# New transfer costs and a new precedence table for a statically scheduled two-block kernel

## The chip, the cores and the metric

The kernel runs on one core of a Trainium2 chip. The metric is the device time of one execution in microseconds (us); the number that counts is the median over runs.

## The reference

Two transformer-like blocks of width 1024 over one sequence of 256 tokens, in float32:

```python
def first_block(x, c, ...):
    mod = silu(c) @ ada_w + ada_b                     # six vectors of 1024
    u = modulate(rmsnorm(x, g), sh_mix, sc_mix)
    p = u @ w_in
    y_conv = conformer_conv(p[..., :1024], ...)       # gated depthwise conv, 31 taps
    y_rwkv = rwkv7_mix(p[..., 1024:], ...)            # 8 heads of 64, a recurrence over the tokens
    x = x + gt_mix * (concatenate([y_conv, y_rwkv]) @ w_out)
    u = modulate(rmsnorm(x, g2), sh_ffn, sc_ffn)
    x = x + gt_ffn * peer_ffn(u, w_q, sub_keys, peer_u, peer_v)
    return rmsnorm(x, final_g)

def peer_ffn(u, ...):     # 8 heads; top 16 of 128 keys twice, top 16 of their 256 sums
    ...                   # picks among 16384 experts with rows in peer_u and peer_v
    h = gelu(einsum('thkd,td->thk', peer_u[expert], u))
    return einsum('thk,thkd->td', softmax(best) * h, peer_v[expert])

def second_block(x, c, ...):
    mod = silu(c) @ w_mod + b_mod
    proj = modulate(rmsnorm(x), ...) @ w_in           # q, k, v of two attentions, an index, gates
    merged = sigmoid(ga) * (dsa(...) @ w_br_dsa) + sigmoid(gb) * (moba(...) @ w_br_moba)
    x = x + gt_m * (merged @ w_out)
    g, up = split(modulate(rmsnorm(x), ...) @ w_gate_up)
    return x + gt_f * ((silu(g) * up) @ w_down)
```

## The kernel before

The program is written as a plain list of operations, and a planner decides where each one stands. `Recorder` notes every operation with the tiles that it reads and writes. `Schedule` is a list scheduler: it plays the five queues PE, ACT, DVE, POOL and DMA forward in model time, gives each operation the duration that `cost` returns, lets its readers become ready after a latency (`latency`, and `DMA_LAT` behind a transfer), and whenever a queue is free takes the ready operation with the highest precedence. Precedence (`bl`) is the length of the longest chain behind the operation in the model, plus its entries in the table `PRIORITY`, one for the stage ("mods3") and one for stage, operation and tile ("mods3 dma_start wraw"), in ns. A positive entry also counts for everything ahead of the operation, a negative one for it alone. The planner also picks the buffer, and for casts and some arithmetic the engine (ACT or DVE, DVE or POOL). What comes out is an order for each queue; the chip then runs each queue in that order, every instruction waiting on semaphores. `build` writes it through one helper line, so every instruction of the program has line 696 in the trace, and rows are told apart by tile names.

All transfers are issued from SP's queue, which is in order too: a transfer that waits for its source or for its buffer holds all those behind it. Four kinds matter below.

- Weights: blocks of 128x1024 floats (512 KB) into `W_wraw`, three buffers (`WRAW = 3`). Each is cast to a rounded high part `W_whi` (on ACT or DVE), the rest goes to `W_wlo` (DVE, seldom POOL), and every product is made of three matmuls. The buffer is free again when `W_wlo` is done.
- Scratch: arrays `scrn0..3` and `scrx0..3` in DRAM, through which the RWKV part rearranges blocks: `scrn` is written from `Ach_AB` in `chunk_first` and read into `Ach_nblk` in `base`; `scrx` is written from `Ach_ublk` in `base` and read into `Arw_XT` in `chunk_mats`.
- Rows: `row_bcast` writes a vector of 1024 that lies as 128x8 in SBUF to DRAM (`row02`, `row05`, `row12`, `row15`, 4 KB each, one element at a time), and reads it back on all partitions. The first, of stage "row", has its source from the modulation stage "mods2".
- Modulation weights: `in_adaR` blocks in the stages "mods2" to "mods4", used directly by matmuls.

In time the stages are: norm, projections and RWKV of block one with the rest of its modulation (0 to 230 us), PEER queries and top-k (`topk`, to some 410), the expert products `hidden` over `peer_u` (to 720), `values` over `peer_v` with the second block's modulation beside them (to 1080), and the second block, whose token-major products `tok_skew` (24 matmuls of 512 columns for two token tiles and one weight block, first one token tile, then the other) stand at its begin and at the begin of its FFN (1285 to 1335).

Of the kernel before, what the change touches and what calls it, by code (L numbers as in the profile page):

```python
# [17 lines left out]
DMA_LAT = 950.0  # L18
# [187 lines left out]
def cost(op, out, reads):  # L206
    n = _free(out)
    if op.eng == "PE":
# [4 lines left out]
        m = _free(lhs)  # L213
# [16 lines left out]
    if op.eng == "DMA":  # L230
        b = P * n * 4
        return b / 358.0 - 8
# [507 lines left out]
def _real(x):  # L740
# [51 lines left out]
    "add C01 scalar_tensor_tensor nsc": -6000.0,  # L792
    "add C01 tensor_mul gtmp": 2500.0,
    "add E00": 35000.0,
    "add E00 tensor_mul gtmp": 82500.0,
    "add E00 tensor_tensor xres": -14000.0,
    "add E01": 3500.0,
    "add E01 scalar_tensor_tensor nsc": -36000.0,
    "add E01 tensor_mul gtmp": -56000.0,
    "add E01 tensor_tensor xres": -145500.0,  # L800
    "attend00 copy ohi": -2000.0,
    "attend00 copy pT": -12000.0,
    "attend00 matmul n": -2000.0,
    "attend00 matmul p": -1000.0,
    "attend00 reciprocal asum": -2000.0,
    "attend00 tensor_mul lg0": -8000.0,
    "attend00 tensor_scalar amax": -3000.0,
    "attend00 tensor_sub olo": 2000.0,
# [3 lines left out]
    "attend01 reciprocal asum": -14000.0,  # L812
# [4 lines left out]
    "attend01 transpose r": 500.0,  # L817
    "attend10 matmul n": -16000.0,
    "attend10 matmul p": -2000.0,
    "attend10 reciprocal asum": 1000.0,  # L820
    "attend10 tensor_reduce amax": -3500.0,
    "attend10 tensor_scalar amax": 16000.0,
    "attend10 tensor_sub olo": -3000.0,
    "attend11 activation lg1": -4000.0,
# [7 lines left out]
    "base": 17500.0,  # L832
    "base dma_start dram": 500.0,
    "base dma_start nblk": -13500.0,
    "base memset ublk": -16000.0,
    "base tensor_mul ublkp": -57000.0,
    "base tensor_reduce ublk": 22500.0,
    "bonus matmul m": -26500.0,
    "bonus tensor_mul av": -1000.0,
    "bonus tensor_scalar av": -4000.0,  # L840
    "consts activation cvec": 40000.0,
    "consts dma_start clevf": -1500.0,
    "consts dma_start cmask": 10000.0,
    "consts dma_start cvec": -16000.0,
    "consts dma_start lorawa": 30000.0,
    "consts dma_start xres": 2000.0,
    "consts iota pj": -125500.0,
    "consts memset bd64": -43000.0,
    "consts memset bdones": -4500.0,
    "consts memset eps": -16000.0,  # L850
    "consts memset o512": -13500.0,
    "consts memset zero": -71000.0,
    "consts tensor_copy clev": -32000.0,
    "consts tensor_scalar ident": 1000.0,
    "consts tensor_scalar omka": 34000.0,
    "conv": -4000.0,
    "conv activation cacc": -18000.0,
    "conv activation convy": 1000.0,
    "conv activation lnr": 1000.0,
    "conv activation tableout": -41000.0,  # L860
    "conv reciprocal lnr": -2000.0,
    "conv tensor_mul cacc": 1500.0,
    "conv tensor_mul lnr": -2500.0,
    "conv tensor_mul lnt": 7000.0,
    "conv tensor_scalar cacc": 9000.0,
    "conv tensor_scalar lnt": -1000.0,
    "conv tensor_scalar lnvv": -41000.0,
    "conv tensor_sub cacc": 1000.0,
    "conv transpose x": 2000.0,
    "ffn activation fsilu": 500.0,  # L870
    "ffn activation ftok": 17000.0,
    "ffn copy whi": -1500.0,
    "ffn dma_start row": -19000.0,
    "ffn dma_start wraw": -4000.0,
    "ffn matmul h": -3000.0,
    "ffn tensor_mul fsilu": -33000.0,
    "ffn tensor_mul ftok": 30500.0,
    "ffn transpose r": -2000.0,
    "ffn0": -500.0,
    "ffn0 dma_start wraw": -15000.0,  # L880
    "ffn0 tensor_tensor wlo": -500.0,
    "ffn1": 500.0,
    "ffn1 copy whi": -15500.0,
    "ffn1 dma_start wraw": -4000.0,
    "ffn1 matmul c": -500.0,
    "ffn1 tensor_tensor wlo": -2000.0,
    "final0": -5000.0,
    "final0 activation f1s": 2000.0,
    "final0 activation f2s": 61000.0,
    "final0 activation mraw": 2000.0,  # L890
    "final0 reciprocal f1r": 3000.0,
    "final0 reciprocal f2r": 6000.0,
    "final0 scalar_tensor_tensor f1t": 32000.0,
    "final0 scalar_tensor_tensor f2t": 36000.0,
    "final0 tensor_add fw": 11000.0,
# [3 lines left out]
    "final0 tensor_scalar f1t": -20000.0,  # L899
    "final0 tensor_scalar f2t": -6000.0,  # L900
    "final0 tensor_scalar xres": -2000.0,
    "final0 tensor_tensor xres": -1000.0,
    "final1 activation f1s": -24000.0,
    "final1 activation f2s": -15500.0,
# [4 lines left out]
    "final1 tensor_mul f1r": 4000.0,  # L909
    "final1 tensor_scalar f1e": -16000.0,  # L910
    "final1 tensor_scalar f1t": -4500.0,
    "final1 tensor_scalar fv": -2000.0,
# [4 lines left out]
    "first0 matmul a": 42000.0,  # L917
    "first0 scalar_tensor_tensor ZR": 4000.0,
    "first0 tensor_mul AB": -12500.0,
    "first0 tensor_mul ZR": -3500.0,  # L920
    "first0 tensor_tensor W": -15000.0,
    "first0 tensor_tensor ZR": 4000.0,
    "first1 dma_start dram": 500.0,
    "first1 matmul b": -39000.0,
    "first1 scalar_tensor_tensor ZR": -1500.0,
    "first1 tensor_mul AB": 8500.0,
    "first1 tensor_mul ZR": -9000.0,
    "first1 tensor_tensor W": -16500.0,
    "first1 tensor_tensor ZR": -4000.0,
    "first2": -9500.0,  # L930
    "first2 dma_start dram": -10500.0,
    "first2 matmul a": 30000.0,
    "first2 scalar_tensor_tensor ZR": -44000.0,
    "first2 tensor_mul AB": -1000.0,
    "first2 tensor_mul ZR": 54500.0,
    "first2 tensor_tensor W": -1000.0,
    "first2 tensor_tensor ZR": 16000.0,
    "first3": 32000.0,
    "first3 dma_start dram": -44500.0,
    "first3 matmul b": -8000.0,  # L940
    "first3 scalar_tensor_tensor ZR": -39500.0,
    "first3 tensor_mul AB": -49500.0,
    "first3 tensor_mul ZR": -4000.0,
    "first3 tensor_tensor W": -12000.0,
    "first3 tensor_tensor ZR": -1000.0,
# [3 lines left out]
    "gn0 activation gsq": 9000.0,  # L949
    "gn0 matmul m": 2000.0,  # L950
    "gn0 reciprocal gnr": -55000.0,
    "gn0 scalar_tensor_tensor yr": -8000.0,
    "gn0 tensor_mul gno": -1000.0,
    "gn0 tensor_mul gnt": -183000.0,
    "gn0 tensor_mul yr": -59500.0,
    "gn0 tensor_scalar gvar": -82000.0,
    "gn0 tensor_sub yr": -12500.0,
    "gn0 transpose m": -56500.0,
    "gn1": 3500.0,
    "gn1 activation gnr": -3000.0,  # L960
    "gn1 activation gsq": -3000.0,
    "gn1 matmul m": -14500.0,
    "gn1 reciprocal gnr": -2000.0,
    "gn1 scalar_tensor_tensor yr": 14500.0,
    "gn1 tensor_mul gno": 32000.0,
    "gn1 tensor_mul yr": 17500.0,
    "gn1 tensor_scalar gnt": 2000.0,
    "gn1 tensor_scalar gvar": -39000.0,
    "gn1 tensor_sub yr": 7500.0,
    "gn1 transpose m": -27500.0,  # L970
    "hidden0 dma_start wraw": -48000.0,
# [3 lines left out]
    "hidden1 copy whi": -4000.0,  # L975
    "hidden1 dma_start wraw": 8000.0,
    "hidden1 matmul h": 3000.0,
    "hidden1 tensor_tensor wlo": 1000.0,
    "hidden2": -1000.0,
    "hidden2 activation gH0": 10000.0,  # L980
    "hidden2 activation gel": -8000.0,
    "hidden2 copy whi": -16000.0,
# [5 lines left out]
    "hidden3 activation gel": -500.0,  # L988
    "hidden3 dma_start wraw": 500.0,
    "hidden3 matmul h": -8000.0,  # L990
# [3 lines left out]
    "hidden4 activation gel": 20000.0,  # L994
    "hidden4 copy whi": 12000.0,
    "hidden4 dma_start wraw": -14000.0,
    "hidden4 matmul h": -29000.0,
    "hidden4 tensor_tensor gH1": 500.0,
    "hidden4 tensor_tensor wlo": 1000.0,
    "hidden5 activation gH1": -2000.0,  # L1000
    "hidden5 matmul h": -16000.0,
    "hidden5 tensor_tensor gH1": 16000.0,
    "hidden6 activation gH1": -7000.0,
# [6 lines left out]
    "hidden7": -2000.0,  # L1010
    "hidden7 activation gH1": 7000.0,
    "hidden7 activation gel": 33000.0,
    "hidden7 copy whi": 9000.0,
    "hidden7 dma_start wraw": 1000.0,
    "hidden7 matmul h": -18500.0,
    "hidden7 tensor_tensor gH1": 17000.0,
    "hidden7 tensor_tensor wlo": 500.0,
    "index copy ki": -18000.0,
# [7 lines left out]
    "index memset kz": 16000.0,  # L1026
# [3 lines left out]
    "index tensor_scalar wi": -2000.0,  # L1030
    "index tensor_sub ropeO": 3000.0,
    "index tensor_tensor ropeB": 6000.0,
    "index transpose r": -16500.0,
    "mats0 copy WT": -20000.0,
    "mats0 copy X": -49000.0,
    "mats0 copy Ylev": -8000.0,
    "mats0 copy_predicated X": 9500.0,
    "mats0 copy_predicated XT": 5000.0,
    "mats0 dma_start XT": 5000.0,
    "mats0 matmul a": -93500.0,  # L1040
    "mats0 transpose a": -32000.0,
    "mats1": -2500.0,
    "mats1 copy WT": -31000.0,
    "mats1 copy X": -134000.0,
    "mats1 copy Ylev": -13500.0,
    "mats1 copy_predicated X": 8500.0,
    "mats1 copy_predicated XT": -36000.0,
    "mats1 dma_start XT": 6000.0,
    "mats1 transpose b": 5500.0,
    "mats2 copy WT": -15000.0,  # L1050
    "mats2 copy X": 26500.0,
    "mats2 copy Ylev": 1000.0,
    "mats2 copy_predicated X": -29000.0,
    "mats2 copy_predicated XT": -22000.0,
    "mats2 dma_start XT": -57000.0,
    "mats2 matmul a": -1500.0,
    "mats2 transpose a": -16000.0,
    "mats3": 8500.0,
    "mats3 copy X": 7000.0,
    "mats3 copy Ylev": 7000.0,  # L1060
    "mats3 copy_predicated X": -39500.0,
    "mats3 copy_predicated XT": -46000.0,
    "mats3 dma_start XT": -30500.0,
    "mats3 matmul b": -56500.0,
    "mats3 transpose b": -4000.0,
    "merge": -1000.0,
    "merge activation tableout": -7000.0,
    "merge copy chi": -14000.0,
    "merge copy whi": -25500.0,
    "merge dma_start wraw": -8000.0,  # L1070
    "merge tensor_add mg": -1000.0,
    "merge tensor_sub clo": -3000.0,
    "merge tensor_tensor wlo": -1000.0,
    "mods2": 1000.0,
    "mods2 copy modrows": -21500.0,
    "mods2 dma_start hraw": -8000.0,
    "mods2 dma_start wraw": 2000.0,
    "mods2 tensor_add mod": -25000.0,
    "mods2 transpose m": 2000.0,
# [1934 lines left out]
```

## Time and profile before

| | |
|---|---|
| median of 3 runs | 1500.91 us (1496.61 to 1501.64) |
| the profiled execution, its own time | 1507.02 us |
| its span, first to last instruction | 1505.2 us |
| PE, PEld, DVE, ACT, POOL busy | 1432.8, 1252.0, 1258.5, 511.3, 97.8 us |
| mean granted TensorE clock | 0.988 |

PE is the matmul engine and PEld its weight loads, which overlap it; DVE, ACT and POOL are the vector, scalar and general engines, SP issues the transfers. A busy time is a union of instruction times; an engine's idle time is put down to what released the instruction behind it. The program names a tile by its region and its name (`W_wraw`, `Arw_XT`); `bank` is PSUM.

### The profile page before, as it was taken

To read this page: it belongs to the slowest core of one execution; us is meant where nothing else is said; L and a number is where in the kernel's file an instruction comes from. 1 tells how busy PE (TensorE), PEld (TensorE's weight loads), DVE (VectorE), ACT (ScalarE), POOL (GpSimd) and SP (SyncE) were. 2 spreads that over 40 slices of the span, in tenths; PEclk is the share of its full clock that TensorE was granted. 3 is DMA by queue.
4 is the path that set the end of the run, shared out by engine and by line. 5 is a ranking of instruction groups with operands and counts; after the bars stand their busy time and mean duration, and the time that the engine had idled before them with its cause. 6 is when DMAs were issued, how large, how long until landed. Compare 5 with 4: busy or idle time off the path is not lost.

```text
span 1505.2 us, 24345 instructions
## 1 busy us (share of the span) xinstructions
PE 1432.8 (95%) x9307; PEld 1252.0 (83%) x9307; DVE 1258.5 (84%) x2395; ACT 511.3 (34%) x917; POOL 97.8 (6%) x91
## 2 busy tenths in 40 slices
PE   7999898998899999999999999999889999899998
PEld 6876666998899999999877888887668899589986
DVE  5798748999999889898879999887988987876676
ACT  2501225243434333232332233322354464533210
POOL 1100000023110000000000000000322100100000
PEclk9999999999999999999999999999999999999999
DMA  9558417544453545545788888786565454765554
GB/s 378 175 148 286 134 45 232 174 153 141 153 169 125 173 154 170 174 162 173 276 258 316 291 300 302 275 287 213 186 211 184 128 166 156 223 209 182 183 184 138
DMA packets 97348, 300.46 MB, mean 200 GB/s; under 512 B 17744, under 2 KB 24528, under 8 KB 97104
## 3 DMA queue, kind: packets, MB, share of 16 engines
q1 hardware_dynamic: 97232, 298.91, 60.4%
q8 instruction: 73, 1.20, 0.3%
q14 instruction: 43, 0.35, 0.1%
HBM read 295.58 MB, written 3.29 MB: 199 GB/s over the span
## 4 chain that ended last, share of the span: by engine, by line
PE 72%; DVE 14%; DMA 9%; ACT 3%; issue 2%; SPq 0%; POOL 0%; DVEq 0%; ACTq 0%; POOLq 0%
PE bank L696 72%; DVE W_wlo L696 4%; DMA W_wraw<-in_peer_v_dram 2%; ACT W_whi L696 1%; DMA W_wraw<-in_w_gua_dram 1%; DVE W_whi L696 1%; DMA row<-A_rowcol 1%; DMA Arw_XT<-scrx 1%; DMA row<-C_rowcol 1%; DVE Ach_ZR L696 1%; DMA W_wraw<-in_w_out_dram 1%; DVE Bt_tv L696 1%; DMA W_wraw<-in_peer_u_dram 1%; DVE Bt_tix L696 1%; DVE Bt_pos L696 1%
## 5 line engine op out<-in xcount | busy, mean ns | idle before, releaser
L696 DVE TENSOR_TENSOR W_wlo<-W_wraw,W_whi 128x1024 fp32r<-128x1024 f32 x417 | 515.8, 1241 | 40.4 <-ACT W_whi L696 21.8
L696 PE MATMUL bank<-X_u2hi,W_wlo 128*128 128x256 f32 x1088 | 295.4, 287 | 8.5 <-DVE W_wlo L696 8.3
L696 ACT CAST W_whi<-W_wraw 128x1024 fp32r<-128x1024 f32 x217 | 227.6, 1050 | 222.7 <-PE bank L696 128.1
L696 PE MATMUL bank<-X_u2hi,W_whi 128*128 128x256 f32 x1088 | 296.7, 287 | 3.6 <-ACT W_whi L696 2.9
L696 PE MATMUL bank<-X_u2lo,W_whi 128*128 128x256 f32 x1088 | 293.7, 285 | 0.0
L696 DVE CAST W_whi<-W_wraw 128x1024 fp32r<-128x1024 f32 x202 | 139.5, 691 | 88.2 <-PE bank L696 60.5
L696 PEld LDWEIGHTS bank<-X_u2hi,W_wlo 128*128 128x128 f32 x1088 | 202.7, 193 | 11.2 <-DVE W_wlo L696 11.1
L696 PEld LDWEIGHTS bank<-X_u2hi,W_whi 128*128 128x128 f32 x1088 | 203.1, 193 | 5.3 <-ACT W_whi L696 4.1
L696 PEld LDWEIGHTS bank<-X_u2lo,W_whi 128*128 128x128 f32 x1088 | 202.9, 193 | 0.0
L696 PE MATMUL bank<-W_whi,A_ah 128*128 128x512 f32 x512 | 139.7, 392 | 6.6 <-DVE W_whi L696 5.6
L696 PE MATMUL bank<-W_wlo,A_ah 128*128 128x512 f32 x512 | 139.9, 392 | 0.0
L696 PE MATMUL bank<-W_whi,A_al 128*128 128x512 f32 x512 | 139.2, 391 | 0.0
L696 PEld LDWEIGHTS bank<-W_whi,A_ah 128*128 128x128 f32 x512 | 96.6, 189 | 28.0 <-issue 6.8
L696 PEld LDWEIGHTS bank<-W_wlo,A_ah 128*128 128x128 f32 x512 | 96.8, 189 | 21.0 <-DVE W_wlo L696 0.9
L696 ACT CAST A_ah<-gH_gH 128x256 fp32r<-128x256 f32 x128 | 51.2, 406 | 184.1 <-PE bank L696 177.9
L696 PEld LDWEIGHTS bank<-W_whi,A_al 128*128 128x128 f32 x512 | 96.7, 189 | 20.5
L696 PE MATMUL bank<-C_chi,W_wlo 128*128 128x256 f32 (+1 forms) x424 | 108.1, 286 | 0.8 <-DVE W_wlo L696 0.7
L696 PE MATMUL bank<-C_chi,W_whi 128*128 128x256 f32 (+1 forms) x424 | 106.6, 284 | 0.0
L696 PE MATMUL bank<-C_clo,W_whi 128*128 128x256 f32 (+1 forms) x424 | 106.2, 284 | 0.0
L696 PEld LDWEIGHTS bank<-C_chi,W_wlo 128*128 128x128 f32 (+1 forms) x424 | 75.0, 188 | 1.7 <-DVE W_wlo L696 1.4
L696 DVE SCALAR_TENSOR_TENSOR A_mraw<-A_mraw,A_cvec 128x1024 f32<-128x1024 f32 x56 | 68.3, 1220 | 8.6 <-DMA A_mraw<-in_wmodT_dram 5.8
L696 PEld LDWEIGHTS bank<-C_chi,W_whi 128*128 128x128 f32 (+1 forms) x424 | 73.6, 187 | 0.8 <-ACT Ca_sg L696 0.2
(433 smaller groups left out, 2167.9 us busy)
## 6 DMA issues: line engine op xcount, KB each, us to landing
W_wraw<-in_peer_u_dram SPq DMA_DIRECT2D x128, 512.0 KB, 3.5
W_wraw<-in_peer_v_dram SPq DMA_DIRECT2D x128, 512.0 KB, 4.6
A_mraw<-in_wmodT_dram SPq DMA_DIRECT2D x48, 512.0 KB, 5.0
W_wraw<-in_w_gu_dram SPq DMA_DIRECT2D x36, 512.0 KB, 4.0
W_wraw<-in_w_down_dram SPq DMA_DIRECT2D x22, 512.0 KB, 4.3
W_wraw<-in_w_out_dram SPq DMA_DIRECT2D x17, 512.0 KB, 4.1
W_wraw<-in_w_gate_dram SPq DMA_DIRECT2D x16, 512.0 KB, 3.6
W_wraw<-in_peer_wqa_dram SPq DMA_DIRECT2D x13, 512.0 KB, 4.3
```

The costliest lines, as they stand in the source:

```text
L696: return getattr(eng, "tensor_copy" if meth == "copy" and e != "ACT" else meth)(*args, **kw)
```

## The change

Two constants of the planner and its table change; no operation of the program is added or removed. The constant latency behind a transfer, `DMA_LAT`, goes from 950 to 1900 ns. A transfer's own time on the DMA queue goes from bytes/358 - 8 ns to bytes/385 ns, and 900 ns more if a tensor whose name begins with `scr` takes part. In `PRIORITY`, which had 655 entries, 348 get another value, 36 go and 81 come: 700 after.

```diff
-DMA_LAT = 950.0
+DMA_LAT = 1900.0
...
     if op.eng == "DMA":
         b = P * n * 4
-        return b / 358.0 - 8
+        small = any(x.tensor.name.startswith("scr") for x in [out] + reads)
+        return b / 385.0 + (900.0 if small else 0.0)
...
-    "base dma_start dram": 500.0,
-    "base dma_start nblk": -13500.0,
+    "base dma_start dram": 49000.0,
+    "base dma_start nblk": 19500.0,
...
-    "mats0 dma_start XT": 5000.0,
+    "mats0 dma_start XT": 27000.0,
...
-    "mods2 dma_start hraw": -8000.0,
+    "mods2 dma_start hraw": -76500.0,
...
-    "mods3 dma_start wraw": -51000.0,
+    "mods3 dma_start wraw": -20000.0,
...
-    "queries dma_start wraw": -16000.0,
+    "queries dma_start wraw": 17000.0,
...
-    "row": -23000.0,
-    "row dma_start dram": -4000.0,
-    "row dma_start row": -64500.0,
+    "row": -26000.0,
+    "row dma_start dram": 28000.0,
...
+    "side dma_start gtf": 500.0,
...
-    "topk0 tensor_copy ijT": -25000.0,
+    "topk0 tensor_copy ijT": -24500.0,
```

## Rows read from the trace of the kernel before

**Rows 1.** The page's first part: busy us (share of the span) and instructions.
```profile
PE 1432.8 (95%) x9307; PEld 1252.0 (83%) x9307; DVE 1258.5 (84%) x2395; ACT 511.3 (34%) x917; POOL 97.8 (6%) x91
```

**Rows 2.** Busy us of each engine by stretch of the span.
```profile
100.00:180.00 80.00, 68.52 (x599) 49.19 (x598) 64.96 (x166) 14.41 (x33) 0.00 (x0) 0.96 0.65 219
263.00:413.00 150.00, 137.23 (x1074) 132.20 (x1073) 144.50 (x467) 56.48 (x70) 32.49 (x21) 0.98 0.48 154
413.00:720.00 307.00, 306.01 (x2785) 303.13 (x2784) 273.66 (x484) 105.70 (x229) 8.36 (x4) 1.00 0.50 163
1078.00:1126.00 48.00, 36.43 (x153) 25.89 (x152) 40.26 (x75) 28.23 (x53) 18.62 (x19) 0.93 0.53 175
1280.00:1335.00 55.00, 47.58 (x197) 32.87 (x198) 46.67 (x64) 26.77 (x44) 4.57 (x3) 1.00 0.70 218
```

**Rows 3.** Transfers by destination and source: count, KB each, median us to landing.
```profile
scrn<-Ach_AB SPq DMA_DIRECT2D x4, 256.0 KB, 4.1
Arw_XT<-scrx SPq DMA_DIRECT2D x4, 256.0 KB, 4.7
...
Ach_nblk<-scrn SPq DMA_DIRECT2D x4, 32.0 KB, 3.3
scrx<-Ach_ublk SPq DMA_DIRECT2D x4, 32.0 KB, 1.9
...
row<-G_mod SPq DMA_DIRECT2D x2, 4.0 KB, 9.5
row<-A_rowcol SPq DMA_DIRECT2D x1, 4.0 KB, 12.0
```

**Rows 4.** The 128 loads of peer_u alone, us to landing.
```profile
DMA to landing us min/median/max: 3.3/3.5/6.8
```

**Rows 5.** PE's waits from 100 to 180 us: us in total, times, longest.
```profile
PE bank L696 <- DMA Arw_XT<-scrx: 4.1, 2, 3.4
...
PE bank L696 <- DMA Afeat_hraw<-in_adaR_dram: 1.9, 1, 1.9
```

**Rows 6.** PE's waits from 360 to 410 us.
```profile
PE bank L696 <- DVE W_wlo L696: 7.0, 5, 4.1
PE bank L696 <- ACT W_whi L696: 2.1, 3, 1.1
```

**Rows 7.** PE's waits from 1078 to 1126 us for weight parts.
```profile
PE bank L696 <- DVE W_wlo L696: 2.3, 5, 0.5
PE bank L696 <- DVE W_whi L696: 0.7, 1, 0.7
```

**Rows 8.** PE's waits from 1280 to 1335 us, the largest.
```profile
PE bank L696 <- DVE W_wlo L696: 3.5, 7, 0.7
```

**Rows 9.** Mean ns of the weight casts, from the page's costliest groups.
```profile
L696 DVE TENSOR_TENSOR W_wlo<-W_wraw,W_whi 128x1024 fp32r<-128x1024 f32 x417 | 515.8, 1241 | 40.4 <-ACT W_whi L696 21.8
L696 ACT CAST W_whi<-W_wraw 128x1024 fp32r<-128x1024 f32 x217 | 227.6, 1050 | 222.7 <-PE bank L696 128.1
```

**Rows 10.** Stretches of the values stage: busy us (instructions), PE first; then the granted clock.
```profile
790.00:827.00 37.00, 35.02 (x147) 28.17 (x146) 34.37 (x49) 10.34 (x18) 0.00 (x0) 0.95 0.89 316
865.00:903.00 38.00, 38.00 (x169) 31.36 (x169) 34.97 (x52) 11.73 (x21) 0.00 (x0) 1.00 0.88 298
```

**Rows 11.** PE's waits in the values stage, 780 to 800 us, then 1045 to 1056 us.
```profile
PE bank L696 <- DVE W_whi L696: 3.1, 2, 2.0
...
PE bank L696 <- DVE W_whi L696: 2.5, 1, 2.5
```

**Rows 12.** Loads of weights issued from 1036 to 1043 us, behind a row: us to landing.
```profile
DMA to landing us min/median/max: 11.5/12.6/12.9
```

**Rows 13.** DVE in order of time: start us, us, instruction.
```profile
364.45 4.22 DVE L696 TENSOR_TENSOR W_wlo<-W_wraw,W_whi 128x1024 fp32r<-128x1024 f32 x2
```

**Rows 14.** SP's issue of the first row write: start us, us.
```profile
163.73 1.03 SPq L696 DMA_DIRECT2D row<-G_mod  x1
```

**Rows 15.** Instructions on G_mod from 100 to 170 us: ns, first and last start.
```profile
L696 DVE TENSOR_TENSOR G_mod<-bank,G_cols x3: 148/167/168, 132.4 to 159.1; 128x8 f32<-128x8 f32 x3
```

More of the change, by code (lines that the diff above doesn't have):

```diff
@@ new lines @@
+    "mats0 dma_start XT": 27000.0,
+    "mats0 matmul a": -13500.0,
+    "mats0 transpose a": 10500.0,
+    "mats1": -6000.0,
+    "mats1 copy WT": -30000.0,
+    "mats1 copy X": 8500.0,
+    "mats1 copy Ylev": 500.0,
+    "mats1 copy_predicated X": 10500.0,
+    "mats1 copy_predicated XT": -10000.0,
+    "mats1 dma_start XT": -22000.0,
+    "mats1 matmul b": -2000.0,
+    "mats1 transpose b": 2500.0,
+    "mats2": 500.0,
+    "mats2 copy WT": -19000.0,
+    "mats2 copy X": 27000.0,
+    "mats2 copy Ylev": 1000.0,
@@ new lines @@
+    "mods2 dma_start wraw": 8500.0,
+    "mods2 tensor_add mod": -39000.0,
+    "mods2 transpose m": -25000.0,
+    "mods3": -18000.0,
+    "mods3 copy modrows": -8000.0,
+    "mods3 dma_start hraw": 10000.0,
+    "mods3 dma_start wraw": -20000.0,
+    "mods3 matmul m": 8000.0,
+    "mods3 tensor_add mod": -500.0,
+    "mods3 transpose m": -47000.0,
+    "mods4": -19000.0,
+    "mods4 copy modrows": 4000.0,
+    "mods4 dma_start hraw": -54500.0,
+    "mods4 matmul m": 17500.0,
+    "mods4 tensor_add mod": -21500.0,
@@ L1096 @@
+    "mods4 transpose m": 40000.0,
+    "norm h0 affine nu": 34000.0,
+    "norm h0 copy chi": 4500.0,
+    "norm h0 tensor_scalar xn": 60000.0,
+    "norm h0 transpose n": 44500.0,
     "norm h1": -1000.0,
@@ new lines @@
+    "norm u0 dma_start mraw1": 27500.0,
+    "norm u0 dma_start wraw": 65000.0,
+    "norm u0 matmul m": 94000.0,
+    "norm u0 matmul w": 38500.0,
+    "norm u0 reciprocal nrr": 9500.0,
+    "norm u0 scalar_tensor_tensor mraw0": 80500.0,
+    "norm u0 scalar_tensor_tensor nrt": 40000.0,
+    "norm u0 scalar_tensor_tensor nsc": 83500.0,
+    "norm u0 tensor_add mod": -29000.0,
+    "norm u0 tensor_scalar nre": -1000.0,
+    "norm u0 tensor_scalar nrt": 18500.0,
+    "norm u0 tensor_scalar nrv": -61500.0,
@@ new lines @@
+    "norm u21 tensor_scalar nrv": 6000.0,
+    "norm u21 tensor_scalar xn": -29000.0,
+    "norm u21 tensor_sub u2lo": 1000.0,
+    "norm u21 transpose u": 3000.0,
+    "norm u4": 8000.0,
+    "norm u4 dma_start hraw": -6500.0,
+    "norm u4 dma_start mraw0": 4000.0,
+    "norm u4 dma_start mraw1": -28000.0,
+    "norm u4 dma_start wraw": -87000.0,
+    "norm u4 matmul m": -36500.0,
+    "norm u4 matmul w": 1500.0,
+    "norm u4 scalar_tensor_tensor mraw0": -16000.0,
+    "norm u4 scalar_tensor_tensor nsc": -33000.0,
@@ new lines @@
+    "norm u4 tensor_add mod": 2000.0,
+    "norm u4 tensor_scalar xn": -38000.0,
+    "norm u4 transpose x": -49000.0,
+    "norm u6": 1000.0,
+    "norm u6 affine u": -1000.0,
+    "norm u6 dma_start hraw": 48000.0,
+    "norm u6 dma_start mraw0": -2000.0,
+    "norm u6 dma_start mraw1": 39000.0,
+    "norm u6 dma_start wraw": 19500.0,
+    "norm u6 matmul m": 6000.0,
+    "norm u6 matmul w": 3000.0,
+    "norm u6 scalar_tensor_tensor nsc": 13000.0,
+    "norm u6 tensor_add mod": -62000.0,
+    "norm u6 tensor_scalar xn": 38500.0,
@@ L1235 @@
-    "prep tensor_scalar kkt": -25000.0,
+    "prep activation sgw": 47000.0,
+    "prep activation sq": 16500.0,
+    "prep activation xs": 52000.0,
+    "prep copy g": 16000.0,
+    "prep dma_start dram": 36000.0,
+    "prep matmul a": 4500.0,
+    "prep matmul b": 4000.0,
+    "prep memset ZR": 32000.0,
+    "prep memset reset": -7000.0,
+    "prep memset sgw": 28000.0,
+    "prep reciprocal kkr": 1500.0,
+    "prep scalar_tensor_tensor av": 1000.0,
+    "prep scalar_tensor_tensor kkn": 19000.0,
@@ L1297 @@
-    "row dma_start dram": -4000.0,
-    "row dma_start row": -64500.0,
-    "second": -9000.0,
-    "second dma_start causal": -16000.0,
+    "queries transpose s": 26500.0,
+    "queries0": -35500.0,
+    "queries0 dma_start wraw": 24500.0,
+    "queries0 matmul c": 32500.0,
+    "queries0 tensor_tensor wlo": 29000.0,
+    "queries1": -18000.0,
+    "queries1 copy whi": 13000.0,
+    "queries1 dma_start wraw": 12000.0,
+    "queries1 matmul c": 17000.0,
+    "queries1 tensor_tensor wlo": 16000.0,
@@ new lines @@
+    "state0 copy yr": 17000.0,
+    "state0 matmul m": 10500.0,
+    "state0 tensor_add yr": -3500.0,
+    "state0 tensor_copy VS": 6500.0,
+    "state0 tensor_tensor S0f": -19000.0,
+    "state1": -3000.0,
+    "state1 copy R": -4000.0,
+    "state1 copy VS": -65500.0,
+    "state1 copy yr": -92000.0,
+    "state1 matmul m": -38000.0,
+    "state1 tensor_add VS": -79000.0,
+    "state1 tensor_add yr": -16000.0,
+    "state1 tensor_copy VS": 4000.0,
+    "state1 tensor_tensor S0f": -4000.0,
+    "state2": -41000.0,
```

684 lines of the change are left out of this document (313 added, 371 removed).

## The prediction

> **What bounds the kernel now.** I read the page's first part first. PE is busy 1432.8 of the span's 1505.2 us [rows 1], so all the time that another order could take away by letting PE wait less is 72.4 us; nothing else in the kernel comes near, since the change removes no instruction. The Trainium skill (Perfetto Trace Analysis, Identifying the Most-Contended Engine) calls the busy share of matmuls a bad measure of headroom and wants that of weight loads; it is 83%, which would leave 253 us of the span [rows 1]. The row of the values stage decides against that reading here: PE has no gap in 865 to 903 us while its weight loads are busy 31.36 of 38 us [rows 10]. So 72.4 us stays the ceiling.
>
> The second view, busy time by stretch, says where the 72.4 us lie [rows 2]. The 307 us of hidden have 1.0 us of PE idle. In 100 to 180 us PE lacks 11.5 us, in 263 to 413 us 12.8, in 1078 to 1126 us 11.6, in 1280 to 1335 us 7.4: 43 us of idle in 333 us of stretches where one stage ends and the next has to fill its buffers. A new order can pay only there. The third view, PE's waits in each of these stretches, names what came last, and this I compare with what the planner believed.
>
> **What the planner believed, part by part.** (1) A 512 KB weight load: 524288/358 - 8 + 950 = 2406 ns before, 524288/385 + 1900 = 3262 ns after. The 128 loads of peer_u land after 3.3 us at the least, 3.5 in the middle [rows 4]. The old number is 0.9 us short, the new one right for a load with little beside it. (2) A 256 KB scratch transfer: 1674 ns before, 681 + 900 + 1900 = 3481 after; the traced ones take 4.1 and 4.7 us. The small block transfers (costed as 128x256): 1308 before, 3140 after; traced 3.3 and 1.9 us [rows 3]. The chain that RWKV's first inverse hangs on is `scrn` written, read, `scrx` written, read: 1674 + 1308 + 1308 + 1674 = 6.0 us before, 13.2 after, traced medians 4.1 + 3.3 + 1.9 + 4.7 = 14.0 us. This is the largest error of the old model, 8 us in one place, and the change mends nine tenths of it. (3) A row write of 4 KB: 4096/358 - 8 + 950 = 953 ns before, 1911 after, because its tensor is named `row`, not `scr`. It takes 9.5 to 12.0 us [rows 3]. This error stays almost whole. The Trainium skill (DMA: Bandwidth & Descriptors, Rules for kernel authors) says that a non-contiguous last dimension becomes one descriptor per element. By that rule the long time follows from the transfer's form, and no place in the order shortens it; the trace agrees with 12.0 us for 4 KB.
>
> **The sum,** each term from PE waits that a transfer or a cast behind it ended; a removed wait is worth its length, bounded by 0 and the whole row.
>
> Scratch and modulation loads, 100 to 180 us: 4.1 (two reads into `Arw_XT`) + 1.9 (an `adaR` load) = 6.0 us [rows 5]. Here the planner was most wrong, other matmuls are at hand to stand in the gap (the modulation products, convolution, out projection), and the table's entries for just these transfers are searched again. I take 4.0, between 0 and 6.0.
>
> Weight parts at the end of top-k, 360 to 410 us: 7.0 + 2.1 = 9.1 us [rows 6]. The longest, 4.1 us, is not a late load: two `W_wlo` took 4.22 us together, against 1241 ns for one, behind the sorting instructions of `topk` that fill DVE (144.50 of 150 us in 263 to 413) [rows 2, 9, 13]. It I leave. Of the other 5.0 I take half, 2.5, since DVE stays as full whatever the order is.
>
> The two token-major starts: 2.3 + 0.7 in 1078 to 1126 us and 3.5 in 1280 to 1335 us, 6.5 us [rows 7, 8]. These are mostly not the order's fault. One `W_wraw` buffer goes round in a landing of 3.5 us, a high part of 1050 ns and a rest of 1241 ns, 5.8 us, so three buffers give a block every 1.93 us [rows 4, 9]. The first pass needs a block for 6 matmuls of 512 columns, and such matmuls run at 38/169 = 0.225 us each [rows 10], 1.35 us. No order loads faster; it can only put other products between. I take 1.5 of 6.5.
>
> Row writes: the waits in the values stage that two of them leave behind, 3.1 + 2.5 = 5.6 us [rows 11]; I take 0, because the planner still thinks them short.
>
> Everywhere else 0: what the longer landing moves in hidden and in the covered part of values lies behind a PE without gaps, and costs only if a load comes later than the buffers allow.
>
> Sum: 4.0 + 2.5 + 1.5 + 0 = 8.0 us. Against the profiled execution, 1507.0 - 8.0 = 1499.0; that execution lay 6.1 us above the median of the runs shown, and the comparison goes by medians: 1500.9 - 8.0 = **1493 us**. All four rows taken whole would be 6.0 + 5.0 + 6.5 + 5.6 = 23.1 us, or 1478 us.
>
> **The rivals.** *No measurable change.* The planner's error was in the landing, but the chip's order already was one that worked: hidden and most of values have no gap, the starts are bound by three buffers, the top-k end by DVE. Then only part of the 6.0 us near the scratch chain comes, and what is won there is lost where the many other entries moved; 1497 to 1505 us. For it speaks that 23.1 us of 1507 is all that the corrected quantities touch; against it that the 6.0 us chain was planned 8 us too short.
>
> *Slower, by the first row write.* Its precedence was -23000 - 4000 = -27 us and becomes -26000 + 28000 = +2 us, 29 us more. Its source can be ready from 132.4 us, when the first of three modulation results is added, and it was issued at 163.73 us [rows 14, 15]. Issued 29 us sooner it falls among the `adaR` loads, which PE reads without a cast between. Loads behind a row write landed after 12.6 us instead of 3.5 [rows 12, 4], 9.1 us late; with some two of slack in the two sets of three buffers PE would stand for about 7 us. The stall also costs behind itself: in 790 to 827 us PE ran 147 matmuls where the undisturbed rate gives 37 x 169/38 = 164.6, so 17.6 x 0.225 = 4.0 us went for the 2.0 us wait seen there, the granted clock being 0.95 [rows 10, 11]. With no gain elsewhere that is 1501 + 7 = 1508 us. It decides if the row write is issued between 135 and 150 us; with the write where it was, or covered by work that has its weights, it costs nothing. Against it: the same move takes it away from the scratch read behind it, which made PE wait 3.4 us [rows 5].
>
> *The change doesn't do what it says.* If the loads that matter are those with others beside them, the new 3262 ns is still short: those behind peer_u's median reach 6.8 us [rows 4]. The order then changes and the waits don't; this ends in the first rival's band.
>
> *A larger gain.* If the search also finds cover for the starts and the top-k end, 15 to 23 us: 1478 to 1486 us.
>
> **How the numbers follow.** A single kernel's runs here spread by 5 us of 1500, so 0.3%, 4.5 us, is about what a measurement can tell from no change. Gain as summed (1487 to 1496 us): 0.40. Larger gain: 0.12. No measurable change: 0.25. Slower by the row write or a like misplacement: 0.23, of it 0.15 up to 1508 us. The likeliest is the sum, 1493 us. To leave out no more than 0.2 I cut the far ends: of the larger gain what lies under 1479 us and of the slower case what lies over 1508 us. Range 1479 to 1508 us; the likeliest case's own is 1487 to 1496. Faster by over 0.3%: 0.40 + 0.12 = 0.52; within 0.3%: 0.25; slower: 0.23.
>
> **What would show it.** Right, step by step: in the changed kernel's trace PE's waits for `Arw_XT` and `adaR` loads between 100 and 180 us fall from 6.0 to about 2 us; the waits for weight parts around the top-k end fall by some 2.5 us; those at the two starts hardly change; PE's busy total stays near 1433 us and its idle falls from 72 to about 64; row writes still take 9 to 12 us and the loads behind them 11 to 13. Wrong: a row write among the `adaR` loads with PE waiting behind it; a longer DVE queue in front of `W_wlo` in 263 to 413 us; or a first stage in which the new entries trade the scratch waits for waits on DVE results, which the landing times say nothing of.

## The result, and the profile after

The change makes the kernel slower: 1508.49 us (1504.88 to 1512.86) against 1500.46 us (1496.61 to 1503.75) of the kernel before beside it, ratio 1.0058, 95% interval 1.0041 to 1.0074. A second comparison gave 1513.77 against 1506.15 us, 1.0045 (1.0029 to 1.0062). The forecast was 1493 us, with a range of 1479 to 1508. The kernel before took 1499.7 to 1500.5 us in the earlier comparisons and 1506.2 to 1506.5 us in the later ones, so what follows compares ratios to the kernel before in the same comparison, and not times across them; 0.001 is 1.5 us. For the same reason a single profile is not enough to place a few microseconds: the execution of the kernel before whose rows stand ahead was a long one (1507.0 us), and a second profile of it is of an execution of 1497.1 us.

The page of the changed kernel shows at first hardly anything; its first part, which answers to [rows 1], and below it that of the second profile of the kernel before:

```profile
PE 1433.9 (95%) x9307; PEld 1249.1 (83%) x9307; DVE 1265.0 (84%) x2410; ACT 490.0 (33%) x903; POOL 91.4 (6%) x90
```

```profile
PE 1430.0 (96%) x9307; PEld 1250.8 (84%) x9307; DVE 1258.6 (84%) x2395; ACT 511.1 (34%) x917; POOL 95.3 (6%) x91
```

PE is as busy as before, in a span of 1506.7 us, so it is idle for 72.8 us. In the second profile of before, with a span of 1495.3 us, it is idle for 65.3. The chain that ended last tells more; its shares by engine, first of before, then of after with its shares by line:

```profile
PE 72%; DVE 14%; DMA 9%; ACT 3%; issue 2%; SPq 0%; POOL 0%; DVEq 0%; ACTq 0%; POOLq 0%
```

```profile
PE 55%; DVE 20%; DMA 13%; issue 8%; ACT 3%; POOL 0%; SPq 0%; DVEq 0%; ACTq 0%; POOLq 0%
PE bank L697 55%; DVE W_wlo L697 8%; DMA A_mraw<-in_wmodT_dram 6%; DMA W_wraw<-in_peer_v_dram 3%; DVE W_whi L697 2%; DMA Afeat_hraw<-in_adaR_dram 1%; DMA A_mraw<-in_adaT_dram 1%; DVE Bt_tix L697 1%; DVE A_al L697 1%; DVE Bt_tv L697 1%; DMA Arw_XT<-scrx 1%; DVE A_mraw L697 1%; ACT W_whi L697 1%; DVE Ach_ZR L697 1%; DVE Bt_pos L697 1%
```

The chain has left PE for 17% of the span, and a transfer that the prediction never named stands third in it: `A_mraw<-in_wmodT`. These are the chunks of the second block's modulation weights, 128x1024 floats each, which are loaded and then multiplied on DVE (`A_mraw<-A_mraw,A_cvec`) beside the values stage. Busy time by stretch of after, which answers to [rows 2] (same work, so shifted by 2 to 6 us) and, last, to the second row of [rows 10]:

```profile
100.00:180.00 80.00, 68.08 (x567) 48.51 (x567) 62.22 (x167) 13.04 (x30) 0.00 (x0) 0.91 0.72 223
265.00:415.00 150.00, 140.05 (x1118) 136.03 (x1117) 147.57 (x474) 57.31 (x70) 35.77 (x21) 0.99 0.47 159
415.00:718.00 303.00, 301.49 (x2747) 298.57 (x2746) 273.38 (x489) 99.68 (x220) 6.92 (x3) 1.00 0.47 164
1082.00:1130.00 48.00, 36.25 (x150) 26.15 (x149) 42.73 (x78) 25.66 (x50) 20.52 (x20) 0.89 0.49 173
1286.00:1341.00 55.00, 49.29 (x228) 36.92 (x229) 52.96 (x74) 23.70 (x44) 0.00 (x0) 1.00 0.69 230
865.00:903.00 38.00, 36.85 (x160) 29.54 (x159) 31.06 (x47) 12.41 (x21) 0.00 (x0) 1.00 0.81 278
```

Top-k lacks 10.0 us of PE instead of 12.8; that was won. The first stretch lacks 11.9 instead of 11.5, at a lower granted clock (0.91 for 0.96). The stretch in the middle of values, which had no gap and 169 matmuls in 38 us, now lacks 1.15 us and has 160. PE's waits of after in the stretches of [rows 5], [rows 6], [rows 7] and [rows 8], in that order:

```profile
PE bank L697 <- DMA Arw_XT<-scrx: 6.6, 2, 5.3
PE bank L697 <- DMA W_wraw<-in_adaR_dram: 1.6, 1, 1.6
PE bank L697 <- DMA Afeat_hraw<-in_adaR_dram: 1.0, 2, 0.8
```

```profile
PE bank L697 <- DVE W_wlo L697: 3.8, 2, 2.7
PE bank L697 <- DVE W_whi L697: 0.9, 1, 0.9
```

```profile
PE bank L697 <- DVE W_wlo L697: 3.6, 4, 1.5
...
PE bank L697 <- DVE W_whi L697: 1.2, 2, 0.7
```

```profile
PE bank L697 <- DVE W_wlo L697: 4.0, 7, 1.5
```

The waits behind scratch and modulation loads rose from 6.0 to 9.2 us, those at the end of top-k fell from 9.1 to 4.7, those at the two starts rose from 6.5 to 8.8. For the values stage two views count that the prediction didn't ask for, waits of DVE and of PE's weight loads from 720 to 1080 us. Before:

```profile
DVE A_mraw L696 <- DMA A_mraw<-in_wmodT_dram: 5.8, 5, 1.8
```

```profile
PEld bank L696 <- DVE W_wlo L696: 0.9, 2, 0.4
```

After:

```profile
DVE A_mraw L697 <- DMA A_mraw<-in_wmodT_dram: 32.4, 19, 5.9
```

```profile
PEld bank L697 <- DVE W_wlo L697: 16.2, 22, 3.5
```

DVE stands 27 us longer for these chunks, and PE's weight loads 15 us longer for the low parts `W_wlo` that DVE makes behind them.

### The profile page after: what moved, and what is told of

Read it like the earlier page. It is cut to its first block, busy times and chain, and to the rows that moved or that the text cites. A ratio compares the mean times of both kernels' runs of the same rounds, so it can differ in the third digit from the quotient of the medians.

```text
span 1506.7 us, 24340 instructions
## 1 busy us (share of the span) xinstructions
PE 1433.9 (95%) x9307; PEld 1249.1 (83%) x9307; DVE 1265.0 (84%) x2410; ACT 490.0 (33%) x903; POOL 91.4 (6%) x90
## 4 chain that ended last, share of the span: by engine, by line
PE 55%; DVE 20%; DMA 13%; issue 8%; ACT 3%; POOL 0%; SPq 0%; DVEq 0%; ACTq 0%; POOLq 0%
PE bank L697 55%; DVE W_wlo L697 8%; DMA A_mraw<-in_wmodT_dram 6%; DMA W_wraw<-in_peer_v_dram 3%; DVE W_whi L697 2%; DMA Afeat_hraw<-in_adaR_dram 1%; DMA A_mraw<-in_adaT_dram 1%; DVE Bt_tix L697 1%; DVE A_al L697 1%; DVE Bt_tv L697 1%; DMA Arw_XT<-scrx 1%; DVE A_mraw L697 1%; ACT W_whi L697 1%; DVE Ach_ZR L697 1%; DVE Bt_pos L697 1%
## 5 line engine op out<-in xcount | busy, mean ns | idle before, releaser
L697 DVE TENSOR_TENSOR W_wlo<-W_wraw,W_whi 128x1024 fp32r<-128x1024 f32 x417 | 509.5, 1227 | 24.0 <-ACT W_whi L697 8.5
L697 ACT CAST W_whi<-W_wraw 128x1024 fp32r<-128x1024 f32 x195 | 204.3, 1049 | 283.9 <-PE bank L697 128.9
L697 DVE CAST W_whi<-W_wraw 128x1024 fp32r<-128x1024 f32 (+1 forms) x224 | 160.8, 718 | 75.0 <-PE bank L697 60.7
L697 PE MATMUL bank<-C_chi,W_whi 128*128 128x256 f32 (+1 forms) x424 | 113.9, 283 | 1.0 <-DVE W_whi L697 1.0
L697 PE MATMUL bank<-C_clo,W_whi 128*128 128x256 f32 (+1 forms) x424 | 113.9, 284 | 0.0
L697 PE MATMUL bank<-C_chi,W_wlo 128*128 128x256 f32 (+1 forms) x424 | 113.1, 285 | 0.5 <-DVE W_wlo L697 0.5
L697 PEld LDWEIGHTS bank<-C_chi,W_whi 128*128 128x128 f32 (+1 forms) x424 | 77.4, 188 | 1.9 <-issue 1.6
```

The source lines that it names most:

```text
L697: return getattr(eng, "tensor_copy" if meth == "copy" and e != "ACT" else meth)(*args, **kw)
```

## Where it lies: experiments that join two orders

The program's operations are the same in both kernels, so an order can be joined from two: up to the first operation of a stage from one plan, from there on from the other, each with its own costs and table. "Hidden" and "values" are the stages.

```diff
-    sch = Schedule(rec)
+    rec, sch = joined(plans, ["values0"], ["new", "old"], regions)                    # new_to_hidden
+    rec, sch = joined(plans, ["values0"], ["old", "new"], regions)                    # new_from_values
+    rec, sch = joined(plans, ["values0", "second"], ["old", "new", "old"], regions)   # new_in_values
```

> The changed kernel's order up to and with hidden, the order of before from values on; every queue's order is spliced at the first product of values. Theory V (the loss sits in values, where the modulation products stand on DVE ahead of W_wlo while their loads are still in flight): 1500 us, ratio 0.998 to 1.002. Theory F (the loss sits in the first stage, where the second read into Arw_XT keeps PE waiting for 5.3 us and the query products start 4.3 us later): 1504 to 1508 us, ratio 1.003 to 1.006.

> The order of before up to and with hidden, the changed kernel's order from values on. Theory V: 1506 to 1508 us, ratio 1.004 to 1.005. Theory F: 1500 us, ratio 0.998 to 1.002. If the two stages share it: both halves near 1504 us.

> The order of before everywhere but in the values stage with the modulation beside it, which is in the changed kernel's order. Theory V (values alone carries the loss): 1507 to 1510 us, ratio 1.004 to 1.007. If the second block carries it too (its profiled steps are 2 us longer): the ratio stays 0.002 or more under the 1.0073 of the order taken over from values to the end.

Measured: the new order up to hidden 1.0014 (0.9995 to 1.0033), no change; from values on 1.0073 (1.0053 to 1.0093); in values alone 1.0095 (1.0068 to 1.0122). So the values stage loses as much as the whole change, or more, and the first part, where the gain was forecast, gives nothing. The profiles show where the first part's gain went. The start times of the matmuls on `X_u2hi` and `A_ah` mark the stages. The first stage, up to the first `X_u2hi`, ends at 234.4 us before and 238.8 after (in the mean 233.5 us in four profiles of the old order and 237.0 in six of the new one); top-k and hidden, from there to the last one, take 484.8 us in the mean of six profiles in the old order and 480.8 in eight in the new one. A gain of 4.0 us follows a loss of about as much. (A joined order also has a seam that neither kernel has; the two parts add to 1.0087 against 1.0058 for the whole, which their intervals allow, so a cost of the seam is neither shown nor excluded.)

The two halves of the change alone:

```diff
 # costs_only: the new costs, the table of before
-DMA_LAT = 950.0
+DMA_LAT = 1900.0
 # table_only: PRIORITY of after, the costs of before
```

> The new transfer costs with the table of before, which was searched for the old costs. Theory C (the costs are right and the new table is what is bad): no slower than 1508 us. Theory M (a table fits only the costs that it was searched with): clearly slower than either kernel, 1520 us or more, since 384 entries are then wrong.

> The new table with the old transfer costs, the counterpart to the new costs with the old table, which took 1532 us. Theory M (a table fits only the costs that it was searched with): 1515 us or more here too. Theory C (the new table is bad whatever the costs): between 1500 and 1510 us, since the costs alone were worse.

Measured: 1.0207 (1.0185 to 1.0230) and 1.0191 (1.0168 to 1.0214). Each half costs 2%, together they cost 0.5%. Each table is a set of corrections to the cost model that it was searched with, and neither fits the other's model; neither half can be called the cause.

## The first stage: the row write in front of another read

SP's issues from 155 to 180 us in after, and below them the landing of the first `Arw_XT` read in it and the wait that it causes:

```profile
155.89 3.56 SPq L697 DMA_DIRECT2D Afeat_hraw<-in_w_out_dram  x3
159.55 0.72 SPq L697 DMA_DIRECT2D row<-G_mod  x1
160.32 1.61 SPq L697 DMA_DIRECT2D W_wraw<-in_w_out_dram  x3
165.74 13.15 SPq L697 DMA_DIRECT2D Arw_XT<-scrx  x2
```

```profile
  PE bank L697: 5.3, 1
...
DMA to landing us min/median/max: 10.4/10.4/10.4
```

Before, the row write stood behind this read (the third of four), at 163.73 [rows 14], and the read landed after 3.8 us; the fourth, behind the row write, after 7.2:

```profile
DMA to landing us min/median/max: 3.8/3.8/3.8
```

```profile
DMA to landing us min/median/max: 7.2/7.2/7.2
```

Now the row write stands 4 us earlier, ahead of three weight loads and the third read, which takes 10.4 us. Three kernels move this one line in SP's queue and nothing else; a fourth does it in the joined order.

```diff
+    row = [op.i for op in ops if op.key == "row dma_start dram"]
+    last = max(key[op.i] for op in ops if op.key == "mats3 dma_start XT")
+    key[row[0]] = (last[0], last[1] + 0.5)        # row_late: behind the fourth read
+    first = min(key[op.i] for op in ops if op.key == "out0 dma_start wraw")
+    key[row[0]] = (first[0], first[1] - 0.5)      # before_row_early: ahead of the w_out loads
```

> The changed kernel, the first row write moved behind the last read into Arw_XT on SP's queue; nothing else differs. If the row write in front of the third of these reads (10.4 us to landing, 3.7 to 4.6 where the row write stands behind it) is why the waits of the first stage didn't fall: PE's waits for Arw_XT from 100 to 180 us fall from 6.6 us to under 2, the time by 3 to 5 us to about 1504 us, ratio 1.002 to 1.004. If the read is late by itself: no change, 1508 us.

> The kernel before, the first row write moved on SP's queue to where the changed kernel has it relative to its neighbours: ahead of three loads of w_out and of the third read into Arw_XT. Nothing else differs. Theory R (the row write's place is what the first stage lost): the third read lands after about 10 us instead of 3.7 to 4.6, PE's wait for Arw_XT from 100 to 180 us rises from 2 to 4 us to 6 or more, the time by 3 to 6 us to 1503 to 1506 us, ratio 1.002 to 1.004. If the first stage's loss came from the rest of its new order: 1500 us.

> The kernel before, the first row write moved behind the fourth read into Arw_XT, one place on SP's queue. Theory R: the fourth read lands after some 3 us instead of 5.6 to 7.2, PE's wait for it goes (2.1 and 3.4 us in the two profiles of before), the time is 1496 to 1499 us, ratio 0.997 to 0.999. If not: 1500 us.

> The changed kernel's order up to and with hidden, the first row write behind the last read into Arw_XT, the order of before from values on. If the parts add (row write -6 us, top-k and hidden -4.7 us by the profiles, the rest of the new first stage at most +3): 1489 to 1495 us, ratio 0.993 to 0.997, faster than both kernels. If the gain of top-k and hidden is noise between executions: 1496 to 1500 us.

Measured: after with the row write late 1.0008 (0.9992 to 1.0024), before with it early 1.0026 (1.0013 to 1.0039), before with it late 0.9955 (0.9935 to 0.9974), the new order to hidden with it late 0.9926 (0.9905 to 0.9947). Four kernels, one line each, and each goes the way of the line: by 4, 7 and 8 us against the kernel that it was made from, and by 13 in the joined order. The three with the write late gained more than was expected. For the kernel before the profile doesn't show where: its first stage ends at 232.5 us, 1.0 earlier than in the old order's mean, and the profiled execution was the longest of its seven. In after with the row write late both reads land in time:

```profile
162.98 6.63 SPq L792 DMA_DIRECT2D Arw_XT<-scrx  x2
169.66 0.50 SPq L792 DMA_DIRECT2D row<-G_mod  x1
```

```profile
DMA to landing us min/median/max: 3.0/3.9/4.7
```

PE's wait for `Arw_XT` in 100 to 180 us is 0.6 us there, 6.6 in after, 8.7 in before with the row write early. What is gained is more than the wait. From 150 to 200 us, in before, in after, in after with the row write late, and in before with it early:

```profile
150.00:200.00 50.00, 43.64 (x428) 35.24 (x428) 34.01 (x87) 16.88 (x31) 0.00 (x0) 0.93 0.32 105
```

```profile
150.00:200.00 50.00, 42.51 (x444) 35.75 (x443) 34.24 (x89) 14.85 (x29) 0.75 (x1) 0.90 0.45 123
```

```profile
150.00:200.00 50.00, 47.60 (x512) 37.18 (x502) 36.84 (x96) 18.21 (x34) 0.76 (x1) 1.00 0.35 114
```

```profile
150.00:200.00 50.00, 39.96 (x403) 32.94 (x394) 29.34 (x76) 13.50 (x25) 0.00 (x0) 0.83 0.42 98
```

The granted clock is 1.00 in the new order where PE didn't stand for this read, and 0.90 and 0.83 where it stood for 5.3 and 7.9 us at a time. With 2.4 GHz and 1.2 GHz as the two levels, 0.90 is 10 of the 50 us at the lower one. The wait isn't all that lowers it: in the order of before it is 0.90 with the row write late too, where PE waits 0.3 us for `Arw_XT`. So the clock's share stays open; the first stage as a whole ends at 227.6 us in the mean of three profiles of the new order with the row write late, and at 237.0 in six with it early.

Does a row write hold up what stands behind it because they share SP's queue? The four row writes were issued from ACT's queue instead, in both kernels:

```diff
-            _emit(eng[e], e, op.meth, args, kw)
+            _emit(nc.scalar if column else eng[e], e, op.meth, args, kw)   # column: a write to row..
```

> The kernel after, but its four writes of a column to scratch (row) are issued from ScalarE's queue instead of SP's, at the same place of the order. If a row write delays what stands behind it because the loads stand in one queue, the third scratch read of the first stage lands in 3-5 us instead of 10.4, loads behind the row writes in the values stage no longer take 11-13 us, the two stalls of PE there (about 5 us each in the order of before) go, and the ratio is 0.994-1.000. If the delay is made in what the queues share (the 16 engines busy with 1024 single elements, memory), the reads behind still take 8-12 us and the ratio stays at 1.004-1.008. A wait of ScalarE for G_mod in front of the write would show as ScalarE idle and PE waits for its casts.

> The kernel before with the same edit (its four row writes issued from ScalarE's queue). If the delay is one of the queue: the first stage gains 0-2 us (its row write already stands behind three of the four scratch reads), the values stage loses its two stalls of PE (about 6 and 1-4 us): ratio 0.993-0.997. If the delay is shared by the queues: 0.999-1.002.

Measured: 1.0040 (1.0018 to 1.0063) and 1.0036 (1.0017 to 1.0054). The theory that the queue alone does it fell: after so edited stays slower than the kernel before, and before so edited becomes slower too. In after so edited, ACT issues the write, and the read that SP issues 4.6 us later still takes 9.2 us, against 10.4 in after and 3.8 in before:

```profile
155.84 0.38 ACTq L698 DMA_DIRECT2D row<-G_mod  x1
```

```profile
160.41 11.98 SPq L698 DMA_DIRECT2D Arw_XT<-scrx  x2
```

```profile
DMA to landing us min/median/max: 9.2/9.2/9.2
```

In before so edited the fourth read, issued 3.7 us behind the write, took 9.6 us. So a write holds up reads of another queue too; by what, these runs don't show. The test isn't quite clean: the first stage of after so edited ends at 232.3 us in its one profile, earlier than in any of the six with the row write early in SP's queue (234.6 to 239.9), and the timed runs gain nothing clear by it.

## The values stage: products in front of casts

In after, SP issues two weight loads and one chunk at a time, over and over, and DVE multiplies a chunk in front of an `A_al` (the low part of the activations) and a `W_wlo`. SP's and DVE's instructions of one such period:

```profile
882.08 2.19 SPq L697 DMA_DIRECT2D W_wraw<-in_peer_v_dram  x2
884.32 0.43 SPq L697 DMA_DIRECT2D A_mraw<-in_wmodT_dram  x1
```

```profile
890.67 1.23 DVE L697 SCALAR_TENSOR_TENSOR A_mraw<-A_mraw,A_cvec 128x1024 f32<-128x1024 f32 x1 [1.60 <-DMA A_mraw<-in_wmodT_dram]
891.82 0.08 DVE L697 DVE_READ_ACCUMULATOR A_mraw<-A_mraw,A_cvec 128x1 f32 x1
891.82 0.42 DVE L697 TENSOR_TENSOR A_al<-gH_gH,A_ah 128x256 fp32r<-128x256 f32 x1
892.16 1.22 DVE L697 TENSOR_TENSOR W_wlo<-W_wraw,W_whi 128x1024 fp32r<-128x1024 f32 x1
```

The chunk is issued third of three in 2.7 us, at 884.32, and its product can't begin before 890.67: 6.35 us. Its landing took 6.3 us of that, which is also the median of the stage's chunks; the planner reckons with 3262 ns from a transfer's turn on its queue. DVE stands for 1.60 us, and the `A_al` and the `W_wlo` behind the product then run without a wait of their own. So the low part comes later, its `W_wraw` buffer is free later, and the next load with it. Three kernels test this. Two move the products on DVE's queue, in opposite directions; the third moves the chunks' loads on SP's queue, one weight load ahead, and leaves DVE's order as it is.

```diff
 # for every modulation product i of the values stage
+    key[i] = (key[behind[0]][0], key[behind[0]][1] + 0.5)  # after_products_later: behind the next W_wlo
+    key[i] = (key[ahead[0]][0], key[ahead[0]][1] - 0.5)    # before_products_earlier: ahead of two W_wlo
 # for every load i of a modulation chunk of the values stage
+    key[i] = (key[ahead[0]][0], key[ahead[0]][1] - 0.5)    # loads_earlier: ahead of one W_wraw load
```

> The changed kernel, every modulation product of the values stage moved behind the next W_wlo on DVE's queue, about 1.6 us later; no other queue differs. Theory V, the wait (DVE holds W_wlo back while it waits for a modulation load that was planned to land after 3.26 us and lands after 6.3): DVE's waits for in_wmodT fall from 32 us to under 12, the values stage from 364 us to 356, the time to 1499 to 1503 us, ratio 0.999 to 1.002. Theory D (the loads themselves, issued three at a time, crowd each other, and DVE's wait only shows it): 1506 us or more, W_wlo or W_whi waiting in the product's place.

> The mirror image: the kernel before, every modulation product moved ahead of the two W_wlo in front of it on DVE's queue, about 3 us earlier; no other queue differs. Theory V, the wait: DVE's waits for modulation loads rise from 6 to 30 us or more and the time to 1506 to 1512 us, ratio 1.004 to 1.008. Theory D: 1500 us, ratio 0.998 to 1.002.

> The kernel after, but in the values stage each load of a modulation chunk A_mraw is issued one W_wraw load earlier on SP's queue; DVE's order, ACT's and PE's stay. If the waiting of VectorE for these chunks is what makes the values stage of the new order 8.7 us longer (no lead between issue and use), DVE's wait for A_mraw from wmodT falls from 32.4 to under 8 us, the 128-matmul steps without a row write return to 29.0 us, the values stage falls from 364 to 355-358 us, and the ratio to the kernel before falls from 1.0058 to 0.999-1.002. Rival one, as with the products moved later: the wait goes, but the two row writes in this stage then cost PE 5 us each more, since the other waits had covered them, and the ratio stays at 1.004-1.006. Rival two: the loads only queue one place earlier and block SP for a free buffer, so that W_wraw lands later: DVE's wait moves to W_whi, ratio 1.006-1.012.

Measured: products later in after 1.0051 (1.0029 to 1.0074); products earlier in before 1.0412 (1.0384 to 1.0440), with 64.6 us of waiting for chunks, a loss at least five times the one expected; loads earlier in after 0.9985 (0.9962 to 1.0009). Products in front of their data do cost, but the first of these alone would have spoken against the cause: DVE's wait fell to 1.9 us and the time didn't move. The loads do move it. Since that number and the change's own come from different comparisons, here are the two kernels in one:

> The kernel after itself, beside the kernel with its modulation loads issued earlier and the kernel before, all on one chip, since the times of before differ by 6 us between the earlier comparisons. The change alone should again stand at 1.004-1.007. If instead it stands at 1.000 or below here, its loss depends on the chip, and the step to 0.9985 seen with the earlier loads was not theirs.

> The kernel after with the loads of modulation chunks in the values stage issued one W_wraw load earlier, beside after itself. If the wait of VectorE for these chunks makes the loss of the values stage, it stands 0.3-0.8% below after (its profiled span was 5.2 us below that of after): 0.997-1.001 of before. If the earlier step was the chip's, the two stand within 0.2% of each other.

Measured: after 1513.77 us, 1.0045 (1.0029 to 1.0062), with the loads earlier 1505.02 us, 0.9984 (0.9969 to 0.9998): 8.75 us between them. Of that pair the middle of the values stage, first after, then with the loads earlier:

```profile
900.00:950.00 50.00, 48.18 (x207) 38.00 (x206) 42.33 (x61) 15.52 (x26) 0.00 (x0) 1.00 0.82 272
```

```profile
900.00:950.00 50.00, 50.00 (x222) 41.43 (x221) 45.79 (x66) 17.27 (x29) 0.00 (x0) 1.00 0.86 296
```

PE has no gap again, as in [rows 10]; DVE's wait for chunks in 720 to 1080 us went from 33.1 to 1.3 us, and values, from the first `A_ah` to the last `A_al`, from 370.9 to 361.5 us. The clock is 1.00 in both, so the difference is PE's standing and not its clock.

One pair of profiles could be chance, but the stage can be cut where the row writes don't reach. It has 1536 matmuls; the seven stretches of 128 from the fourth to the tenth lie between the row writes. Together they take 203.1 to 204.0 us in seven profiles of the old order, 207.7 to 214.6 in six of the new one, and 203.1 in all three with the loads earlier. The loss is in these stretches, and the loads' place takes it away. The other five stretches, at the stage's ends and behind the row writes, take 152.3 to 159.2 us in the old order and 156.7 to 160.6 with the loads earlier. That is why a single profile's whole stage says little: with both repairs, below, it is 363.7 us, as long as in after, though the seven stretches are as short as before.

The products moved back on DVE also bring the seven stretches to 203.5 us, from 211.0 in after; in the same profile the other five take 160.0 us instead of 153.1. This fits the rival named for the earlier loads, that the row writes then cost more because the other waits had covered them. But the five stretches vary by as much within one order, so why that kernel's time didn't move stays open.

Both repairs together:

> The kernel after with both repairs: modulation loads one W_wraw load earlier on SP's queue in the values stage, and the first row write behind the last scratch read of the first stage. If the two losses are separate and each has its cause here, the ratio is that of the row write alone (1.0008) less the 5-8 us of the values stage: 0.995-0.998. If the values stage gives nothing back (the row writes there take over), it stays at 1.000-1.002.

Measured: 1493.89 us beside 1506.38, 0.9902 (0.9878 to 0.9927). This is the changed order with two kinds of transfer moved, and it beats both kernels, by more than was expected. Not all of that is the change's own gain. The row write moved late alone brings the kernel before to 0.9955, and what earlier chunk loads would do in the order of before was not tried. Like beside like there is one pair, in one comparison and both with the row write late: the new order to hidden took 1496.55 us and the order of before 1500.84, so the first part of the change is worth about 4 us once this write is out of its way.

## Why the prediction was wrong, step by step

- **Scratch and modulation loads, -4.0 us.** The step that failed first. These waits rose by 3.2 us, from 6.0 to 9.2. The planner did know the 14 us chain better, but the row write, still costed at 1.9 us, came to stand ahead of the third read. With the row write late the new order's first stage ends at 227.6 us, against 233.5 in four profiles of the old order and 232.5 in the one of before with the row write late. So a gain of the term's size was there, 5 to 6 us, though a stage's length is not these waits alone. A smaller part of the waits has another place: the second of the four reads, with three weight loads issued just ahead of it, lands after 6.8 to 8.6 us in the new order, and after at most 5.8 in the old one; with the row write late, 0.6 to 1.7 us of waiting for `Arw_XT` is left.
- **The row-write rival.** Its mechanism decided, but not at its place. The write was issued at 159.55, not between 135 and 150 us, and its victim was not an `adaR` load but the next scratch read. The sentence set against the rival, that the move takes the write away from the scratch read behind it, looked at the fourth read and forgot the third. That its sum, 1508 us, is the measured time is luck: it counted one stall of 7 us and nothing else, and what was measured is a loss of some 3.5 us in the first stage, a gain of 4.0 in top-k and hidden and a loss of 7.5 in values (stage means of the profiles).
- **End of top-k, -2.5 us.** The right way, and too small: waits 4.4 us less, the two stages 4.0 us shorter.
- **Token-major starts, -1.5 us.** The waits that it named didn't shrink, they rose (6.5 to 8.8 us). PE's idle time in the two stretches fell from 19.0 to 17.5 us, just the 1.5 forecast, but by other waits: that is luck.
- **Row writes, 0.** The planner did go on believing them short, as the term says, and where their landing shows in the two profiles of after they still took 10.6 and 12.2 us. But 0 was wrong in effect, since the change moved one, as above.
- **"Everywhere else 0".** The second step that failed, and in the sum of stages the larger one: values 359.0 us in the mean of six profiles of the old order, 366.5 in five of the new. The argument was that a later landing costs only if it exceeds what the buffers allow, and PE had no gap. It looked at PE's transfers alone. DVE, 35 us busy in 38 [rows 10], takes its work in order, and a modulation product that waits for its own load holds the casts behind it. What the change moves in a covered stretch had to be asked of each queue that feeds it.
- **The ceiling of 72 us** came from one profile; the second one of before leaves 65 us. That PE's busy time would stay and its idle time decide held: 1433.9 us busy, and 72.8 idle instead of a forecast 64. The losses are gaps of PE, in the first stage beside a lower clock.

The losses don't add up exactly. After with the row write late stands at 1.0008 although its values stage has the long wait still (31.2 us). The two repairs, 0.0050 and 0.0061, would bring the change from 1.0051, the mean of its two comparisons, to 0.994, and both together gave 0.9902 (0.9878 to 0.9927). This sum takes ratios from different comparisons; the difference, 0.004, stays unexplained.

## What to carry to other kernels

A planner's cost that is mended in one place can make a neighbour's error count: after the change list the transfers whose cost is still wrong (here the 4 KB column write, planned at 1.9 us and measured at 8 to 15) and see what now stands behind each. In a stretch without PE gaps look at the in-order engines that feed it: the slack between a load's landing and its use on DVE is as much of a margin as PE's. A misplaced instruction is found by moving that one line on that one queue, and a repair that removes a wait is only believed when the time moves.

## Of the hardware

In these profiles a write of 4 KB as 1024 single elements took 8.0 to 14.9 us to land. A third or fourth `Arw_XT` read of 256 KB, issued 4 to 7 us behind it, landed after 5.2 to 12.2 us; one with the write still to come took 3.0 to 4.7. Reads were late with the write in the same queue (10.4) and in ACT's (9.2). A 512 KB load issued as the third within 2.7 us landed after 6.3 us, where the loads of peer_u took 3.5 in the median [rows 4]. The stretch of the first stage with a wait of PE of 5.3 or 7.9 us had a granted clock of 0.90 or 0.83, and one with a wait of 0.3 us for the same reads had 0.90 as well; 1.8 us of gaps in 50 us of values left it at 1.00.
